# A transformer block on one core: the third mixer's centring, gates and norm logarithms written another way

## The chip, the core and the metric

The kernel runs on one core of a Trainium2 chip (trn2). The metric is the device time of one launch in microseconds, the median of several runs. A profile comes from one further execution of its own.

## The reference

One layer of a hybrid block on 256 tokens of width 2048, in float32. Cut to what matters here:

```
u = rms_norm(x) ; proj = u @ w_in              # q,k,v of two attentions, r,k,v and low ranks of the third mixer, 3 gates
y_a = stick_breaking_attention(...) ; y_b = forgetting_attention(...)
# third mixer: 16 heads of 64, per head and token a 64 x 64 state
kk    = k*k_k / max(sqrt(sum((k*k_k)**2)), 1e-12)          # norm over a head's 64 features
decay = exp(-exp(w_log)) ; a = sigmoid(a0 + ad @ a_up)
state = state*decay - (state @ kk)*(kk*a) + v*k            # token after token
y     = state @ r
y     = (y - mean(y)) * rsqrt(var(y) + eps) * ln_w + ln_b + bonus*v     # mean and var over the 64 features
m = g_a*(y_a @ P_a) + g_b*(y_b @ P_b) + g_c*(y_c @ P_c) ; x = x + rms_norm(m @ w_out)
x = x + rms_norm(relu(rms_norm(x) @ w_up)**2 @ w_down)
```

The subtraction of the mean over a head's features is linear, so the kernel applies it to v before the recurrence: a product of v with `cen`, the 128 x 128 matrix I - 1/64 inside each head's block.

## The kernel before

**Weights.** All weight matrices stream through SBUF as tiles of 128 x 1024 (`wraw`, L160; three buffers `raw`). Each tile is cut into a rounded high half `whi`, written by ScalarE (L173), and a low half `wlo`, the difference, written by VectorE (L175); three buffers each. TensorE multiplies both halves (`gemm`, L187, with lines L191, L195, L197; `tok`, L208, with lines L235 and L220), so every weight tile needs one step on each of the two vector engines before TensorE can read it. A rounded operand has the type fp32r ("hl", "whi", "cr" in the rows), an unrounded one f32; a product of unrounded operands stands in the trace as two passes of the same line, one of rounded operands as one. Activations are cut the same way by `split` (L253; ScalarE L256, VectorE L257). After a projection ScalarE moves half of a sum out of PSUM (L697) and VectorE adds the other half (L698).

**The mixer runs between the weight products.** The three mixers are one generator. Each `yield` gives a cost in vector time. `tick` (L137) is called once or twice in each weight tile, adds SHARE times its argument to a credit, and `step` (L116) runs pieces of the generator while the credit is positive. A plain number or ("go", cost) lets the next piece follow at once if credit is left. ("stage", cost, hold) ends the tick and lets nothing follow for `hold` ticks: it stands where TensorE's next products need what the vector engines have just been given. TensorE's order is the order in which this code calls it. The order of ScalarE, VectorE and GpSimd is made by the tile scheduler.

**The third mixer** (`rwkv_half`, L725) runs twice, for four pairs of heads each. In its order:

- sums of squares of k for the norm, two groups of two pairs (L745, L746, product `heads` in L100 and L101); of each group VectorE takes the maximum (L760), ScalarE the logarithm (L761) and the exponential (L762), each with a table load ahead of it; then five VectorE steps of a Newton correction (L764 to L769);
- `gates` (L776) for each pair: low-rank products (L783), three ScalarE steps (L791 to L793), VectorE's scan over the tokens of a chunk into `cs` (L794), two exponentials of it (L797 `ep`, L798 `em`), and operands for the recurrence on VectorE and GpSimd (L802 to L822);
- products per pair (L836, L840) and their masks (L845);
- centring of v (L857): per pair four products of 64 x 128 with unrounded v as the stationary and `cen` as the moving operand, 64 columns wide, in two column halves of the array;
- a triangular inverse on VectorE, 31 short pairs of steps between transposes (L876 to L893);
- the recurrence over four chunks (L928 to L964) and the head norm.

The constants lie in three tiles: `ident`; `cr`, which ScalarE writes rounded from `ones` (L447); and `con`, unrounded. `cen` lay in `con`.

Of the kernel before, what the change touches and what calls it, by code (L numbers as in the profile page):

```python
# [21 lines left out]
AHEAD = 1  # L22
SHARE = 0.88
HALF = 1024
# [18 lines left out]
_c = 0  # L43
for _n, _w in (("ident", 128), ("ones", 128), ("bones", 128), ("trig", 128), ("mst", 128),
               ("madd", 128), ("cen", 128), ("scm", 128), ("scan", 256)):
    CC[_n] = (_c, _w)
    _c += _w
NCON = _c
NR = 384


@with_exitstack
def hybrid_block(ctx, tc, xt, x, gains, params, consts, lora, gup, wst, out):
# [41 lines left out]
    def CR(name):  # L95
        c0 = CC[name][0] - 128
        return cr[:, c0:c0 + 128]
# [624 lines left out]
    def heads(ps, hi, lo):  # L722
        twice(ps, CR("bones"), *(t.rearrange("p a b -> p (a b)") for t in (hi, lo)))

    def rwkv_half(hf):  # L725
# [27 lines left out]
        for hi, lo in hls:  # L753
            pss.append(mps())
            heads(pss[-1], hi, lo)
        for i2, ps in enumerate(pss):
            ri = B6[:, 2 * i2:2 * i2 + 2, :]
            sc = B6[:, 4:6, :]
            sq = rp.tile([128, 2, T], F32, tag="AX", name=nm("sq"), bufs=5)
            V.tensor_scalar(sq, ps.rearrange("p (a b) -> p a b", a=2), 1e-24, None, ALU.max)  # L760
            A.activation(sc, sq, AF.Ln, scale=float(2.0 ** 20))  # L761
            A.activation(ri, sc, AF.Exp, scale=-0.5)  # L762
            yield 0.6
            V.tensor_scalar(ri, ri, 1024.0, None, ALU.mult)  # L764
# [11 lines left out]
        def gates(i, p):  # L776
# [16 lines left out]
            A.activation(lw, lw, AF.Identity, scale=CE, bias=cst[:, 0:1])  # L793
            V.tensor_tensor_scan(c, C("scan"), lw, 0.0, ALU.mult, ALU.add)  # L794
            c4 = c.rearrange("p (c t) -> p c t", c=4)
            G.memset(ep[:, :, 0:1], 1.0)
            A.activation(ep[:, :, 1:65], c4, AF.Exp)  # L797
            A.activation(em, c, AF.Exp, scale=-1.0)  # L798
            G.tensor_copy(ecol[:, i, :], ep[:, :, 64])
            yield 0.8  # L800
            kp = g1()
# [23 lines left out]
        for i, p in enumerate(PR):  # L825
# [25 lines left out]
            yield ("stage", 1.9, 3.5 if i == 0 else 2.0)  # L851

        pss = [mps(), mps()]
        for i, p in enumerate(PR):
            for cc in range(4):
                o = 256 * (i % 2) + 128 * (cc // 2)
                PE.matmul(pss[i // 2][64 * (cc % 2):64 * (cc % 2) + 64, o:o + 128], done[f"v{p}"][:, cc * 64:cc * 64 + 64],  # L857
                          C("cen"), start=True, stop=True)
        for i, p in enumerate(PR):
# [852 lines left out]
```

## Time and profile before

| | us |
|---|---|
| median of 3 runs (lowest to highest) | 1504.24 (1503.12 to 1506.56) |
| the profiled execution's own time | 1505.64 |
| its span, first to last instruction | 1503.8 |
| TensorE busy | 1489.7 |
| VectorE busy | 1206.8 |
| ScalarE busy | 938.4 |
| GpSimd busy | 91.1 |
| granted TensorE clock, mean of the span | 0.998 |

The third mixer's first half lies between about 200 and 410 us of the span, its second between about 427 and 660 us. In a timeline row the columns are start, length, engine, line, operation, operands, shape, count, and in brackets idle time just before and what ended it. A group's row ends in total busy time, mean ns of one, and idle time before. PE is TensorE, PEld its weight loads, DVE VectorE, ACT ScalarE, POOL GpSimd.

### The profile page before, as it was taken

The numbers are of one execution on the slowest core, as the hardware profiler recorded it, in microseconds if no ns is written. First come the engines' busy times: TensorE is split into PE (matmuls) and PEld (weight loads), VectorE is DVE, ScalarE is ACT, GpSimd is POOL, SyncE is SP. The second block draws the span as 40 slices with busy tenths as digits, with TensorE's granted clock in tenths as the row PEclk, the third lists the DMA queues.
The fourth block names the chain that finished last, engine by engine and source line by source line (L and its number), as shares of the span: only waits on it lengthen the run. The fifth ranks groups of instructions, "written<-read, shape, count | busy, mean of one in ns | idle before, by whom it ended". The sixth has DMA issues, their size and how long they took to land.

```text
span 1503.8 us, 22719 instructions
## 1 busy us (share of the span) xinstructions
PE 1489.7 (99%) x8384; PEld 1250.7 (83%) x8384; DVE 1206.8 (80%) x1677; ACT 938.4 (62%) x1435; POOL 91.1 (6%) x151
## 2 busy tenths in 40 slices
PE   9999999999999999999999999999999999999997
PEld 7888888887788887788888888888888888888886
DVE  7965679895688796476657788999899989999996
ACT  7665677545776445564445776776767666767663
POOL 0011003000001000000000000000000000000000
PEclk9999999999999999999999999999999999999999
DMA  8545445454445455345674768879888888889874
GB/s 284 202 150 178 151 158 169 155 182 162 157 167 173 150 192 189 135 165 195 226 243 161 261 179 256 252 223 286 243 269 239 225 279 258 249 259 261 256 216 149
DMA packets 107055, 312.19 MB, mean 208 GB/s; under 512 B 12352, under 2 KB 14400, under 8 KB 106944
## 3 DMA queue, kind: packets, MB, share of 16 engines
q1 hardware_dynamic: 96336, 279.35, 54.8%
q0 software_dynamic: 8064, 29.36, 10.5%
q10 hardware_dynamic: 2544, 2.03, 0.5%
q8 instruction: 66, 1.08, 0.3%
q14 instruction: 45, 0.37, 0.1%
HBM read 279.24 MB, written 2.10 MB: 187 GB/s over the span
## 4 chain that ended last, share of the span: by engine, by line
PE 94%; DVE 2%; ACT 1%; issue 1%; DMA 0%; SPq 0%; POOLq 0%; DVEq 0%; POOL 0%; ACTq 0%
PE gps L235 27%; PE gps L191 22%; PE gps L195 12%; PE gps L220 7%; PE mps L1430 3%; PE mps L1432 3%; PE mps L1431 3%; PE gps L1432 2%; PE gps L1430 2%; PE gps L1431 2%; PE gps L197 2%; DVE wlo L175 1%; PE mps L836 1%; PE gps L359 1%; PE gps L1219 1%
## 5 line engine op out<-in xcount | busy, mean ns | idle before, releaser
L175 DVE TENSOR_TENSOR wlo<-raw,whi 128x1024 fp32r<-128x1024 f32 x570 | 691.3, 1223 | 151.5 <-ACT whi L173 141.8
L173 ACT ACTIVATE whi<-raw 128x1024 fp32r<-128x1024 f32 x570 | 597.9, 1057 | 246.5 <-PE gps L235 71.7
L191 PE MATMUL gps<-pk,whi 128*128 128x512 f32 x1460 | 370.7, 392 | 1.0 <-ACT whi L173 0.8
L191 PEld LDWEIGHTS gps<-pk,whi 128*128 128x128 f32 x1460 | 270.6, 188 | 56.4 <-ACT whi L173 1.7
L235 PE MATMUL gps<-whi,pk 128*128 128x512 f32 x1004 | 253.5, 392 | 0.0
L195 PEld LDWEIGHTS gps<-pk,wlo 128*128 128x128 f32 x1561 | 212.8, 190 | 15.4 <-DVE wlo L175 0.5
L235 PEld LDWEIGHTS gps<-whi,pk 128*128 128x128 f32 x1004 | 186.4, 188 | 40.0 <-issue 1.0
L195 PE MATMUL gps<-pk,wlo 128*128 128x256 f32 x1561 | 218.0, 282 | 0.1
L235 PE MATMUL gps<-wlo,pk 128*128 128x512 f32 x502 | 138.1, 393 | 0.1
L235 PEld LDWEIGHTS gps<-wlo,pk 128*128 128x128 f32 x502 | 93.1, 188 | 20.0 <-DVE wlo L175 0.5
L1347 ACT ACTIVATE tmp<-gps 128x256 f32<-128x256 f32 x64 | 24.6, 385 | 105.2 <-PE gps L197 103.3
L1430 PE MATMUL mps<-whi,fm 128*128 128x512 f32 x224 | 88.6, 396 | 1.4 <-ACT whi L173 1.3
L1431 PE MATMUL mps<-whi,fm 128*128 128x512 f32 x224 | 87.7, 392 | 0.0
L1432 PE MATMUL mps<-wlo,fm 128*128 128x512 f32 x224 | 87.4, 390 | 0.0
L1410 POOL DMA_DIRECT2D raw<-raw x56 | 48.8, 872 | 571.9 <-DVE raw L1407 279.8
L1407 DVE TENSOR_TENSOR raw<-raw,raw 128x1024 f32<-128x1024 f32 x56 | 68.4, 1222 | 0.8
L1430 PE MATMUL gps<-whi,fm 128*128 128x512 f32 x168 | 65.8, 392 | 0.0
L1432 PE MATMUL gps<-wlo,fm 128*128 128x512 f32 x168 | 65.7, 391 | 0.0
L1431 PE MATMUL gps<-whi,fm 128*128 128x512 f32 x168 | 65.5, 390 | 0.0
L220 PE MATMUL gps<-whi,pk 128*128 128x512 f32 x224 | 60.8, 393 | 0.0
L1430 PEld LDWEIGHTS mps<-whi,fm 128*128 128x128 f32 x224 | 42.3, 189 | 9.7 <-ACT whi L173 3.5
L1432 PEld LDWEIGHTS mps<-wlo,fm 128*128 128x128 f32 x224 | 42.1, 188 | 9.4
(358 smaller groups left out, 1743.0 us busy)
## 6 DMA issues: line engine op xcount, KB each, us to landing
raw<-in_wst_dram SPq DMA_DIRECT2D x510, 512.0 KB, 4.3
raw<-raw POOLq DMA_DIRECT2D x56, 512.0 KB, 7.2
x<-in_xt_dram SPq DMA_DIRECT2D x8, 256.0 KB, 5.6
x<-in_x_dram SPq DMA_DIRECT2D x8, 256.0 KB, 5.5
raw<-in_wst_dram SPq DMA_DIRECT2D x6, 256.0 KB, 4.9
pk<-in_wst_dram SPq DMA_DIRECT2D x6, 256.0 KB, 5.1
g<-in_gains_dram SPq DMA_DIRECT2D x4, 256.0 KB, 5.0
pk<-in_gains_dram SPq DMA_DIRECT2D x4, 256.0 KB, 6.8
```

What stands on the lines that cost most here:

```text
L173: A.activation(hi, raw, AF.Copy)
L175: low = lambda: V.tensor_tensor(lo, raw, hi.bitcast(F32), ALU.subtract)
L191: PE.matmul(ps, hi[:, i * 128:i * 128 + 128], pks[i], start=first and i == 0, stop=False)
L195: PE.matmul(ps[:, 0:T], lo[:, i * 128:i * 128 + 128], pks[i][:, 0:T], start=False, stop=False)
L197: PE.matmul(ps, hi[:, (n - 1) * 128:n * 128], pks[n - 1], start=False, stop=True)
L220: PE.matmul(ps[tt], pks[k][:, c:c + 128], w[:, (k - k0) * 512:(k - k0) * 512 + 512], start=k == 0 and part == 0 and w is hl[0], stop=w is ...
L235: PE.matmul(ps[tt], pks[k][:, c:c + 128], w[:, (k - k0) * 512:(k - k0) * 512 + 512], start=k == 0 and part == 0 and w is hl[0], stop=False)
L1407: V.tensor_tensor(R[d, a], R[d, a], R[d, b], ALU.add)
L1410: G.dma_start(out=R[d, a], in_=R[d, b], accum_op=ALU.add)
L1430: PE.matmul(Q[f], a, w, start=d == d0 and i == 0, stop=False)
L1431: PE.matmul(Q[f], b, w, start=False, stop=False)
L1432: PE.matmul(Q[f], a, wl, start=False, stop=d == dn and i == 1)
```

## The change

Five edits in one:

1. SHARE goes from 0.88 to 0.93.
2. `cen` moves from the unrounded constants into the rounded tile, which grows from 384 to 512 columns.
3. Centring splits v of the four pairs into rounded high and low parts (L256, L257; one "go" or "stage" each), and multiplies both by the rounded `cen`: per pair four products of 128 x 128 over the array's full width, instead of four unrounded ones of 64 columns' width.
4. The norm takes the logarithms of both groups in one piece, the exponentials in the next, with a "stage" behind each, then both corrections.
5. In `gates` a "stage" of 0.7 stands between the scan and the exponentials; the 0.8 behind the exponentials is gone.

```diff
-SHARE = 0.88
+SHARE = 0.93
...
-NR = 384
+NR = 512
...
+        sc, sqs = B6[:, 4:6, :], []
         for i2, ps in enumerate(pss):
-            ri = B6[:, 2 * i2:2 * i2 + 2, :]
-            sc = B6[:, 4:6, :]
             sq = rp.tile([128, 2, T], F32, tag="AX", name=nm("sq"), bufs=5)
             V.tensor_scalar(sq, ps.rearrange("p (a b) -> p a b", a=2), 1e-24, None, ALU.max)
-            A.activation(sc, sq, AF.Ln, scale=float(2.0 ** 20))
-            A.activation(ri, sc, AF.Exp, scale=-0.5)
-            yield 0.6
+            A.activation(B6[:, 2 * i2:2 * i2 + 2, :], sq, AF.Ln, scale=float(2.0 ** 20))
+            sqs.append(sq)
+        yield ("stage", 1.0, 1)
+        A.activation(B6[:, 0:2, :], B6[:, 0:2, :], AF.Exp, scale=-0.5)
+        A.activation(B6[:, 2:4, :], B6[:, 2:4, :], AF.Exp, scale=-0.5)
+        yield ("stage", 0.1, 1)
+        for i2, sq in enumerate(sqs):
+            ri = B6[:, 2 * i2:2 * i2 + 2, :]
...
             V.tensor_tensor_scan(c, C("scan"), lw, 0.0, ALU.mult, ALU.add)
+            yield ("stage", 0.7, 0.7)
...
             G.tensor_copy(ecol[:, i, :], ep[:, :, 64])
-            yield 0.8
...
+        vs = []
+        for p in PR:
+            t = pair()
+            split(done[f"v{p}"], t.rearrange("p a b -> p (a b)"))
+            vs.append(t)
+            yield ("stage" if p == PR[3] else "go", 0.4, 2)
         pss = [mps(), mps()]
-        for i, p in enumerate(PR):
-            for cc in range(4):
-                o = 256 * (i % 2) + 128 * (cc // 2)
-                PE.matmul(pss[i // 2][64 * (cc % 2):64 * (cc % 2) + 64, o:o + 128], done[f"v{p}"][:, cc * 64:cc * 64 + 64],
-                          C("cen"), start=True, stop=True)
+        for i, t in enumerate(vs):
+            for b in range(2):
+                o = 256 * (i % 2) + 128 * b
+                for a in range(2):
+                    PE.matmul(pss[i // 2][:, o:o + 128], t[:, a, 128 * b:128 * b + 128], CR("cen"), start=a == 0,
+                              stop=a == 1)
```

The edits move the lines behind them: L761 and L762 of before are L760 and L763/L764 now, L797 is L802, L802 is L806, L857 is L868, L888 is L899, L893 is L904.

**Where ScalarE stands with the logarithms of the first half.** Before, the first group's (`sq_399`), around the high half `whi_418`; the second group's follow two high halves later:

```order
L173 ACTIVATE whi_409_2167<-raw_408_2165 128x1024
L699 ACTIVATE zp_403_2133<-tmp_402_2132,par_74 128x256
L761 ACT_TABLE_LOAD
L761 ACTIVATE b6_374_2037<-sq_399_2124 128x512
L173 ACTIVATE whi_418_2205<-raw_417_2203 128x1024
L762 ACT_TABLE_LOAD
L762 ACTIVATE b6_374_2037<-b6_374_2037 128x512
L697 ACTIVATE tmp_413_2194<-gps_404_2139 128x256
L173 ACTIVATE whi_421_2230<-raw_420_2228 128x1024
```

Now, both groups' between two high halves:

```order
L173 ACTIVATE whi_407_2144<-raw_406_2142 128x1024
L760 ACT_TABLE_LOAD
L760 ACTIVATE b6_374_2027<-sq_399_2114 128x512
L760 ACTIVATE b6_374_2027<-sq_400_2117 128x512
L763 ACT_TABLE_LOAD
L763 ACTIVATE b6_374_2027<-b6_374_2027 128x512
L764 ACTIVATE b6_374_2027<-b6_374_2027 128x512
L697 ACTIVATE tmp_402_2133<-gps_390_2073 128x256
L173 ACTIVATE whi_410_2171<-raw_409_2169 128x1024
```

The two groups' loads and steps were two pieces with high halves between and behind them; they are one piece now.

**ScalarE at the first pair's gates**, from the second group's logarithm or from the high half that takes its place. Before:

```order
L761 ACT_TABLE_LOAD
L761 ACTIVATE b6_374_2037<-sq_411_2177 128x512
L762 ACT_TABLE_LOAD
L762 ACTIVATE b6_374_2037<-b6_374_2037 128x512
L791 ACTIVATE lw_427_2256<-mps_425_2242,wah_123 128x256
L792 ACTIVATE tha_429_2258<-mps_426_2243,wah_123 128x256
L793 ACTIVATE lw_427_2256<-lw_427_2256,cst_116 128x256
L802 ACTIVATE g1_432_2279<-tha_429_2258,oka_124,wah_123 128x256
L697 ACTIVATE tmp_437_2291<-gps_416_2202 128x256
L797 ACTIVATE ep_431_2260<-cs_428_2257 128x4x64
L798 ACTIVATE em_430_2259<-cs_428_2257 128x256
L173 ACTIVATE whi_445_2324<-raw_444_2322 128x1024
```

Now:

```order
L173 ACTIVATE whi_442_2302<-raw_441_2300 128x1024
L795 ACTIVATE lw_427_2256<-mps_425_2242,wah_123 128x256
L796 ACTIVATE tha_429_2258<-mps_426_2243,wah_123 128x256
L797 ACTIVATE lw_427_2256<-lw_427_2256,cst_116 128x256
L806 ACTIVATE g1_432_2279<-tha_429_2258,oka_124,wah_123 128x256
L697 ACTIVATE tmp_437_2291<-gps_416_2202 128x256
L802 ACTIVATE ep_431_2260<-cs_428_2257 128x4x64
L803 ACTIVATE em_430_2259<-cs_428_2257 128x256
L173 ACTIVATE whi_446_2329<-raw_445_2327 128x1024
```

The second group's logarithm and exponential have left the piece; the exponentials of the scan (`cs`) stand behind the same step, L697, as before.

**VectorE at the end of the first triangular inverse**, up to the same weight tile (its low half is `wlo_691` before and `wlo_695` now; `Ti` and `tp` are the inverse's). Before:

```order
L175 TENSOR_TENSOR wlo_688_3475<-raw_686_3472,whi_687_3474 128x1024
L881 TENSOR_TENSOR tp_608_3042<-U_606_3040,Ti_607_3041 64x175
L883 TENSOR_TENSOR Ti_607_3041<-Ti_607_3041,tp_608_3042 64x7x25
L881 TENSOR_TENSOR tp_608_3042<-U_606_3040,Ti_607_3041 64x156
L883 TENSOR_TENSOR Ti_607_3041<-Ti_607_3041,tp_608_3042 64x6x26
L698 TENSOR_TENSOR tmp_681_3462<-gps_671_3402,tmp_680_3461 128x256
L881 TENSOR_TENSOR tp_608_3042<-U_606_3040,Ti_607_3041 64x135
L883 TENSOR_TENSOR Ti_607_3041<-Ti_607_3041,tp_608_3042 64x5x27
L175 TENSOR_TENSOR wlo_691_3494<-raw_689_3491,whi_690_3493 128x1024
```

Now:

```order
L175 TENSOR_TENSOR wlo_692_3488<-raw_690_3485,whi_691_3487 128x1024
L894 TENSOR_TENSOR Ti_611_3053<-Ti_611_3053,tp_612_3054 64x3x29
L892 TENSOR_TENSOR tp_612_3054<-U_610_3052,Ti_611_3053 64x60
L894 TENSOR_TENSOR Ti_611_3053<-Ti_611_3053,tp_612_3054 64x2x30
L892 TENSOR_TENSOR tp_612_3054<-U_610_3052,Ti_611_3053 64x31
L894 TENSOR_TENSOR Ti_611_3053<-Ti_611_3053,tp_612_3054 64x31
L899 STREAM_TRANSPOSE TW_679_3447<-Ti_611_3053 32x16x32 x2
L698 TENSOR_TENSOR tmp_685_3475<-gps_675_3418,tmp_684_3474 128x256
L904 STREAM_TRANSPOSE SC_423_2240<-Ti_611_3053 32x16x32
L175 TENSOR_TENSOR wlo_695_3508<-raw_693_3505,whi_694_3507 128x1024
```

The inverse is further on by four of its pairs of steps at this tile, and three of the four transposes behind it stand ahead of the low half.

4 lines of the change are left out of this document (2 added, 2 removed).

## The prediction

> **What bounds the kernel now.** I read the page's busy line first, then the chain that ended last, then TensorE's timeline for places where it stands still.
>
> ```profile
> PE 1489.7 (99%) x8384; PEld 1250.7 (83%) x8384; DVE 1206.8 (80%) x1677; ACT 938.4 (62%) x1435; POOL 91.1 (6%) x151
> PE 94%; DVE 2%; ACT 1%; issue 1%; DMA 0%; SPq 0%; POOLq 0%; DVEq 0%; POOL 0%; ACTq 0%
> ```
>
> TensorE is busy for 99% of the span and carries 94% of the chain. A change in the mixer can therefore act in three ways only: through the time its own products take on TensorE, through the few places where TensorE waits for a weight half, or by creating new ones. The profiled execution took 1505.64 us (span 1503.8 and 1.84 around it), 1.40 above the 1504.24 median of three runs. I work out differences and put them on the median. A measurement of this kernel tells about 0.2%, 3.0 us, from no change.
>
> The timeline of TensorE around 226 us shows the one clear wait inside the mixer's time. Columns are start, length, engine, line, operation.
>
> ```profile
> 200.69 0.40 PE L197 MATMUL gps<-pk,whi 128*128 128x512 f32 x1
> 200.93 1.32 PE L191 MATMUL gps<-pk,whi 128*128 128x512 f32 x5
> ...
> 219.71 2.00 PE L191 MATMUL gps<-pk,whi 128*128 128x512 f32 x8
> 221.55 1.12 PE L195 MATMUL gps<-pk,wlo 128*128 128x256 f32 x8
> ...
> 225.07 0.39 PE L197 MATMUL gps<-pk,whi 128*128 128x512 f32 x1
> 226.00 2.11 PE L191 MATMUL gps<-pk,whi 128*128 128x512 f32 x8 [0.54 <-ACT whi L173]
> 228.22 1.21 PE L195 MATMUL gps<-pk,wlo 128*128 128x256 f32 x8
> ```
>
> Undisturbed, L197 is followed by L191 after 0.24 us and eight L191 take 1.84. Here they take 0.93 and 2.22: TensorE loses 0.69 + 0.38 = 1.07 us. ScalarE before it:
>
> ```profile
> 216.44 1.28 ACT L761 ACT_TABLE_LOAD   x1
> 218.61 1.28 ACT L762 ACT_TABLE_LOAD   x1
> 219.91 0.63 ACT L762 ACTIVATE b<-b 128x512 f32<-128x512 f32 x1
> 224.27 0.42 ACT L797 ACTIVATE ep<-cs 128x256 f32<-128x256 f32 x1 [1.85 <-DVE cs L794]
> 224.91 1.04 ACT L173 ACTIVATE whi<-raw 128x1024 fp32r<-128x1024 f32 x1
> ```
>
> From 216.44 to 224.91 ScalarE makes no high half: two table loads, log and exponential of the second pair group, three tanh steps, and 1.85 us of standing still at L797 for VectorE's scan. Three buffers of whi do not cover 8.5 us. In the second half the same place costs less:
>
> ```profile
> 453.48 1.98 PE L235 MATMUL gps<-whi,pk 128*128 128x512 f32 x8
> 455.30 1.07 PE L235 MATMUL gps<-wlo,pk 128*128 128x512 f32 x4
> 456.20 1.98 PE L235 MATMUL gps<-whi,pk 128*128 128x512 f32 x8
> 458.25 1.21 PE L235 MATMUL gps<-wlo,pk 128*128 128x512 f32 x4
> ```
>
> Eight high products take 1.82, and 2.05 the second time; the four low ones also run 0.14 longer: 0.37 us, with VectorE late.
>
> **The change part by part.**
>
> *Logs in one step, gates in two.* The table loads and the wide steps are counted by these groups:
>
> ```profile
> L761 ACT ACT_TABLE_LOAD x4 | 5.1, 1283 | 0.1
> L762 ACT ACT_TABLE_LOAD x4 | 5.1, 1283 | 0.1
> ```
>
> Each half loses one load at L761 and one at L762, 4 x 1.283 = 5.1 us of ScalarE in all. In the new order both logs and both exponentials stand three high halves earlier as one block: 2 x 1.28 + 4 x 0.55 (the 0.63 at 219.91 less the overlap with the next) = 4.8 us without a high half, then L697. The block of 8.5 us falls to the three tanh steps, L806, L697, a wait for the scan and two exponentials, about 4 us. TensorE takes 2.72 us a tile (453.48 to 456.20 in the rows above), and beside the tile in use two more fit the three buffers, 5.4 us: both blocks fit into that, so the 1.07 us should go. If ScalarE enters the first block less than 4.8 us ahead, that block shows instead. The step between scan and exponential does not do what its name says at the first gate: in the order nothing but L697 stands between, so L802 can still wait for the scan, with one high half queued behind it. It has less ahead of it. In the second half, VectorE no longer waits for an exponential at the first operation of the second group, so I count the 0.37 as gone too. Term: **-1.4**, bounds 0 and -1.5; a loss is left out, since the same steps run with fewer loads.
>
> The Trainium skill, page "ScalarE: Activation LUTs", section "Table sets: the hidden batching unit", speaks against this part: one set holds log and exponential, so a log followed by an exponential needs one load. By it the grouping would remove no load, the block would stay, and the sum would be 1.4 us higher. The rows decide: every log and every exponential here has its own load of 1283 ns.
>
> *Centring.* The row of the old products, with their neighbours, and two neighbours of the new ones:
>
> ```profile
> 280.19 1.30 PE L191 MATMUL gps<-pk,whi 128*128 128x512 f32 x5
> 281.43 1.97 PE L857 MATMUL mps<-con,g 128*64 128x128 f32 x32
> 283.32 0.73 PE L191 MATMUL gps<-pk,whi 128*128 128x512 f32 x2
> 283.90 1.10 PE L195 MATMUL gps<-pk,wlo 128*128 128x256 f32 x8
> 284.83 0.40 PE L191 MATMUL gps<-pk,whi 128*128 128x512 f32 x1
> ...
> 241.62 0.66 PE L840 MATMUL mps<-ident,At 128*128 128x128 f32 x4
> 242.03 0.36 PE L100 MATMUL mps<-hl,cr 128*128 128x256 f32 x1
> ```
>
> Old, per half: 16 products of full precision in 32 passes, 281.43 to 283.32, 1.89 us. Entering and leaving the 64-wide form costs 0.10 (five L191 in 1.24 against 5 x 0.227, 1.82 / 8 above) and 0.13 (two in 0.58 against 0.45): 2.12. New: 16 rounded products, 128 wide, 128 columns, nothing to enter. No row shows that form. Below stands half of L195, which has the same weights and 256 columns: 0.93 / 8 = 0.116, halved 0.058, 0.93 us in all. Above stands the old price of a full-width product, two 64-wide ones of two passes: 1.89 / 8 = 0.236, 3.78 us. Nearest are L195 itself and the one-pass 128-column L840, 0.41 / 4 = 0.103; both load 128 columns of weights each time. I take 0.11: 1.76 us, a gain of 0.36 per half. Term: **-0.7**, bounds -2.4 and +3.3.
>
> *Work added for it.* Four copies and four differences per half:
>
> ```profile
> L256 ACT ACTIVATE pk<-g 128x256 fp32r<-128x256 f32 x8 | 3.0, 404 | 0.9 <-DVE g L1005 0.9
> L257 DVE TENSOR_TENSOR pk<-g,pk 128x256 fp32r<-128x256 f32 x8 | 3.3, 418 | 0.5 <-ACT pk L256 0.5
> ```
>
> ScalarE gets 8 x 0.404 = 3.2 us, less than the loads it loses. VectorE gets 4 x 0.418 = 1.7 us per half, just ahead of the triangular inverse, where it has no room. TensorE's centring group stands behind the last difference, which the order puts ahead of the low half of the tile where TensorE meets the group; a tile's 2.72 us covers it, and without that cover the next weight tile would wait behind the group. How full VectorE is:
>
> ```profile
> 278.00:336.00 58.00, 58.00 (x398) 50.03 (x397) 56.56 (x109) 29.76 (x47) 0.59 (x6) 1.00 0.48 163
> 511.00:571.80 60.80, 60.80 (x295) 50.05 (x294) 58.54 (x105) 27.77 (x38) 0.00 (x0) 1.00 0.48 161
> ```
>
> The columns after the length are TensorE, weight load, VectorE, ScalarE: VectorE is busy for 97% and 96% of the two inverses.
>
> *The larger share.* At 0.93 the mixer's steps come 5.7% sooner, counted in weight tiles, and TensorE's mixer groups move by at most two tiles. The total of mixer work is the same, so nothing is gained at the end, where TensorE has gate products to do anyway. But inside an inverse more VectorE work falls between two low halves. I added the rows of VectorE's order between low halves, at the durations of their lines in the trace: up to the tile whose low half is wlo_691 before and wlo_695 now, VectorE has been given 6.6 us more since the gates, as three transposes now stand ahead of it. Three tiles later all but 1.3 of it is given back.
>
> ```profile
> L888 DVE STREAM_TRANSPOSE TW<-Ti 32x512 f32<-32x512 f32 x4 | 4.6, 1188 | 0.0
> L893 DVE STREAM_TRANSPOSE SC<-Ti 32x512 f32<-32x512 f32 x8 | 8.7, 1083 | 0.1
> ...
> 277.89 1.29 DVE L845 TENSOR_TENSOR SC<-mps,con 128x512 f32<-128x512 f32 x2 [1.05 <-PE mps L836]
> ...
> 325.36 1.21 DVE L175 TENSOR_TENSOR wlo<-raw,whi 128x1024 fp32r<-128x1024 f32 x1
> ...
> 328.43 1.07 PE L235 MATMUL gps<-wlo,pk 128*128 128x512 f32 x4
> ```
>
> Three transposes are 3.4 us of the 6.6. Against it stand the idle time of 1.05 us ahead of the inverse, which can be filled, and TensorE's group of L836, which lies one tile earlier, so that VectorE begins the inverse 2.7 us sooner: 2.85 us are left. Today that low half (325.36) is done at 326.57 and first read at 328.43, 1.86 us ahead. So TensorE waits 2.85 - 1.86 = 1.0 us: **+1.0**, bounds 0 (a step that ScalarE or a buffer held up anyway) and 6.6 - 1.86 = 4.7 (nothing of the idle time can be used). The second inverse has more idle time ahead of it, from 475 to 510 us:
>
> ```profile
> DVE wlo L175 <- ACT whi L173: 7.7, 5, 1.9
> ```
>
> Five gaps of 7.7 us in all can take the extra, and I count nothing there. Vector steps outside the inverses, the 64 KB more of rounded constants and GpSimd, at 6%, cost nothing: idle time of those engines covers them.
>
> Sum: 1505.64 - 1.4 - 0.7 + 1.0 = 1504.5 for such an execution; on the median 1504.24 - 1.1 = **1503.1**.
>
> **The rivals.** *VectorE becomes the bound in both inverses* (slower). For it: 97% busy, and a low half only 1.86 us ahead. Against it: the extra is transient. It decides where the idle time and the earlier start can't be used: then the first inverse costs 4.7 by itself, 1504.24 - 1.4 - 0.7 + 4.7 = 1506.8, and 1511.5 if the second costs as much again.
> *Small rounded products cost two passes.* For it: every unrounded product here does. Against: L195 and L840. 1504.24 - 1.4 + 3.3 + 1.0 = 1507.1.
> *They cost what their columns cost*, 0.058 to 0.08. For it: L195 costs half of L191 (0.116 against 0.227), so columns set the price there. Against: L840. With 0.07: 2 x (2.12 - 1.12) = 2.0, and no wait in the inverse: 1504.24 - 1.4 - 2.0 = 1500.8. The Trainium skill, page "TensorE: Matmul & The Clock Gate", section "Back-to-back issue gap", gives about 81 ns for 128 columns in a stream of loads and products; by it the gain of this term would be 2 x (2.12 - 1.30) = 1.6 us, an estimate. No run here shows that form.
> *The step does not part scan and exponential*, and the 1.07 us wait stays, at this tile or another, so that only the 0.37 goes. For it: the order, where L802 still follows L697. Against: the block ahead of it is gone. 1504.24 - 0.4 - 0.7 + 1.0 = 1504.1.
>
> **How the numbers follow.** Forecast (1501.6 to 1504.6) 0.42; VectorE bound 0.17, two passes 0.12, cost by columns 0.13, no parting 0.16. The range leaves out the outer part of the VectorE rival and a little at each end of the others: 1500.4 to 1507.2. Faster by over 0.2% (below 1501.2): most of the column rival and a tail of the forecast, 0.17. Slower (above 1507.2): half of the VectorE rival and of the two-pass one, and a little for a wait that I did not see, 0.17. The rest, 0.66, lies within.
>
> **What would show it.** L191 after L197 near 226 us at 0.24 and no `<-ACT whi` there; four table loads fewer, two each at the new lines; the centring group at 1.7 to 1.8 us for 16 records, 0.9 or 3.8 for the rivals; low halves in the first inverse read within 1 us of their end, with TensorE idle `<-DVE wlo L175` near 325 to 335. Wrong would be TensorE waits of over 1 us anywhere between 280 and 570, or a mixer group that waits for its operands.

## The result and the profile after

The changed kernel takes 1507.64 us (median of 12 runs, 1506.05 to 1512.30), the kernel before 1504.57 beside it (12 runs, 1503.12 to 1507.51). The ratio is **1.0021**, 95% interval 1.0011 to 1.0031: 3.1 us slower, where 1.1 us faster was forecast, and 0.4 us above the range. The profiled execution took 1508.15 us with a span of 1506.4, against 1505.64 and 1503.8 before.

The busy line of the page hardly moves. TensorE's waits do: a list of them, with the microseconds in all, the number and the longest.

```profile
PE 1489.8 (99%) x8352; PEld 1250.0 (83%) x8352; DVE 1209.1 (80%) x1685; ACT 934.7 (62%) x1439; POOL 88.0 (6%) x151
...
PE gps L235 <- DVE wlo L175: 2.0, 2, 1.7
PE mps L467 <- DVE a L462: 1.2, 1, 1.2
```

The kernel before has neither of the two waits. I price each wait by starts: the time from one product's start to the next, less what the same pair takes undisturbed. TensorE at the start, near 226 us and near 458 us:

```profile
35.12 0.39 PE L197 MATMUL gps<-pk,whi 128*128 128x512 f32 x1
36.75 0.70 PE L467 MATMUL mps<-a,cr 128*128 128x256 f32 x2 [1.24 <-DVE a L462]
...
225.68 0.40 PE L197 MATMUL gps<-pk,whi 128*128 128x512 f32 x1
225.91 2.00 PE L191 MATMUL gps<-pk,whi 128*128 128x512 f32 x8
227.75 0.52 PE L195 MATMUL gps<-pk,wlo 128*128 128x256 f32 x3
...
457.57 1.07 PE L235 MATMUL gps<-wlo,pk 128*128 128x512 f32 x4
458.48 1.98 PE L235 MATMUL gps<-whi,pk 128*128 128x512 f32 x8
460.30 1.07 PE L235 MATMUL gps<-wlo,pk 128*128 128x512 f32 x4
```

L191 follows L197 after 0.23 us near 226, and the eight take 1.84: the 1.07 us are gone. At 458 the eight high products take 1.82 and the four low ones 0.91: the 0.37 us are gone too. ScalarE ahead of the first of these places:

```profile
216.90 1.06 ACT L173 ACTIVATE whi<-raw 128x1024 fp32r<-128x1024 f32 x1 [0.77 <-DMA raw<-in_wst_dram]
222.49 0.42 ACT L802 ACTIVATE ep<-cs 128x256 f32<-128x256 f32 x1 [1.58 <-DVE cs L798]
223.12 1.05 ACT L173 ACTIVATE whi<-raw 128x1024 fp32r<-128x1024 f32 x1
```

It still stands still for 1.58 us at L802 for the scan, where it was 1.85: the new step hardly parts scan and exponential at the first gate. But the stretch without a high half is 5.2 us long (217.96 to 223.12) instead of 8.5, as the second group's logarithm and exponential have left it. At the start L467 begins 1.63 us after L197, where it took 0.24 before (35.95 to 36.19): 1.39 us new. VectorE there, after and then before; L462 adds up the squares that L467 reads:

```profile
33.64 0.69 DVE L462 TENSOR_TENSOR a<-a 128x512 f32<-128x512 f32 x1
34.86 1.23 DVE L175 TENSOR_TENSOR wlo<-raw,whi 128x1024 fp32r<-128x1024 f32 x1 [0.54 <-ACT whi L173]
36.01 0.69 DVE L462 TENSOR_TENSOR a<-a 128x512 f32<-128x512 f32 x1
```

```profile
34.12 1.48 DVE L462 TENSOR_TENSOR a<-a 128x512 f32<-128x512 f32 x2
35.52 1.22 DVE L175 TENSOR_TENSOR wlo<-raw,whi 128x1024 fp32r<-128x1024 f32 x1
```

The last addition now stands behind one more low half, which itself waits for its high half. The centring, the first inverse, the second group of logarithms and the second inverse on TensorE:

```profile
279.41 1.54 PE L191 MATMUL gps<-pk,whi 128*128 128x512 f32 x6
280.79 1.90 PE L868 MATMUL mps<-cr,hl 128*128 128x128 f32 x16
282.52 0.69 PE L191 MATMUL gps<-pk,whi 128*128 128x512 f32 x2
283.05 1.11 PE L195 MATMUL gps<-pk,wlo 128*128 128x256 f32 x8
...
326.57 1.98 PE L235 MATMUL gps<-whi,pk 128*128 128x512 f32 x8
330.24 1.19 PE L235 MATMUL gps<-wlo,pk 128*128 128x512 f32 x4 [1.69 <-DVE wlo L175]
...
436.76 1.07 PE L235 MATMUL gps<-wlo,pk 128*128 128x512 f32 x4
438.17 2.11 PE L235 MATMUL gps<-whi,pk 128*128 128x512 f32 x8 [0.34 <-ACT whi L173]
...
539.98 1.07 PE L220 MATMUL gps<-whi,pk 128*128 128x512 f32 x4
541.23 0.73 PE L220 MATMUL gps<-wlo,pk 128*128 128x512 f32 x2 [0.19 <-DVE wlo L175]
...
565.74 1.54 PE L235 MATMUL gps<-whi,pk 128*128 128x512 f32 x6
567.64 1.20 PE L235 MATMUL gps<-wlo,pk 128*128 128x512 f32 x4 [0.35 <-DVE wlo L175]
```

The sixteen rounded products take 1.73 us from 280.79 to 282.52. The six before them take 1.38 instead of 1.36, the two behind 0.53 instead of 0.45: 1.83 in all, against 2.12. The eight products at 326.57 last 3.67 us until the next start instead of 1.81: 1.86 lost, and 0.37 is lost at another low half of this inverse, near 305: 2.23 in all. Near 437 it is 1.41 instead of 0.91, in the second inverse 1.25 instead of 0.91 and 1.90 instead of 1.36.

The sum: 1.39 + 2.23 + 0.50 + 0.88 new, 1.07 + 0.37 removed, 2 x 0.29 for the centring, **+2.98 us**. The spans differ by 2.6 and the medians by 3.07. That the three agree so closely is partly luck. From the products just ahead of L467 to the end of the mixer the changed trace loses 3.8 us, 0.8 more than this list holds; and the two traces also differ by 0.8 us in the first 35 us (less now), by 1.1 near 1200 us (less now) and by 0.8 between 1310 and 1360 us (more now), which I can't put down to any edit. The list tells where most of the time in the mixer went, not yet which part of the change sent it there.

### The profile page after: what moved, and what is told of

Read it like the earlier page. It is cut to its first block, busy times and chain, and to the rows that moved or that the text cites. A ratio compares the mean times of both kernels' runs of the same rounds, so it can differ in the third digit from the quotient of the medians.

```text
span 1506.4 us, 22659 instructions
## 1 busy us (share of the span) xinstructions
PE 1489.8 (99%) x8352; PEld 1250.0 (83%) x8352; DVE 1209.1 (80%) x1685; ACT 934.7 (62%) x1439; POOL 88.0 (6%) x151
## 4 chain that ended last, share of the span: by engine, by line
PE 88%; DVE 6%; issue 2%; ACT 2%; DMA 1%; ACTq 0%; SPq 0%; DVEq 0%; POOLq 0%; POOL 0%
PE gps L235 23%; PE gps L191 21%; PE gps L195 12%; PE gps L220 6%; PE mps L1441 3%; PE mps L1442 3%; PE mps L1443 3%; DVE wlo L175 3%; PE gps L1443 2%; PE gps L1441 2%; PE gps L1442 2%; PE gps L197 1%; DVE tp L892 1%; DMA raw<-in_wst_dram 1%; DVE Ti L894 1%
## 5 line engine op out<-in xcount | busy, mean ns | idle before, releaser
L191 PE MATMUL gps<-pk,whi 128*128 128x512 f32 x1460 | 370.1, 392 | 0.2 <-ACT whi L173 0.2
L191 PEld LDWEIGHTS gps<-pk,whi 128*128 128x128 f32 x1460 | 270.5, 188 | 55.3 <-ACT whi L173 0.9
L195 PEld LDWEIGHTS gps<-pk,wlo 128*128 128x128 f32 x1561 | 212.6, 190 | 16.1 <-DVE wlo L175 1.3
L195 PE MATMUL gps<-pk,wlo 128*128 128x256 f32 x1561 | 218.2, 282 | 0.2 <-DVE wlo L175 0.2
```

Source lines behind the costliest of these rows:

```text
L191: PE.matmul(ps, hi[:, i * 128:i * 128 + 128], pks[i], start=first and i == 0, stop=False)
L195: PE.matmul(ps[:, 0:T], lo[:, i * 128:i * 128 + 128], pks[i][:, 0:T], start=False, stop=False)
```

## The experiments

My theory had three parts: the start's wait comes from the place of the centring matrix among the constants, the waits in the inverses from the larger share, and the edits on logarithms and gates are a gain. The rival put the waits in the inverses down to the work that the centring adds to VectorE. Neither held fully. Each run has its own runs of the kernel before on the same chip; medians in us:

| run | this | before | ratio, 95% interval |
|---|---|---|---|
| b_const | 1505.50 | 1503.67 | 1.0013 (1.0004 to 1.0022) |
| b_share93 | 1509.22 | 1503.67 | 1.0037 (1.0025 to 1.0050) |
| b_cen | 1516.82 | 1503.67 | 1.0087 (1.0073 to 1.0101) |
| share88 | 1514.85 | 1503.67 | 1.0075 (1.0063 to 1.0088) |
| b_lg | 1502.01 | 1504.37 | 0.9982 (0.9973 to 0.9991) |
| a_sep | 1507.09 | 1504.37 | 1.0020 (1.0011 to 1.0029) |
| free88 | 1506.89 | 1504.37 | 1.0020 (1.0012 to 1.0029) |
| a_sep_pool | 1506.60 | 1504.37 | 1.0017 (1.0008 to 1.0025) |
| b_lg93 | 1510.04 | 1504.41 | 1.0038 (1.0025 to 1.0051) |
| a_sep_free88 | 1506.01 | 1504.41 | 1.0012 (1.0004 to 1.0021) |
| a_sep_pool_free88 | 1506.19 | 1504.41 | 1.0013 (1.0004 to 1.0022) |
| a_sep_pool90 | 1506.85 | 1504.41 | 1.0019 (1.0010 to 1.0027) |
| b_lg_splits | 1501.78 | 1504.20 | 0.9989 (0.9979 to 0.9998) |
| t_noyield88 | 1506.30 | 1504.20 | 1.0019 (1.0010 to 1.0028) |
| t_blg_h1 | 1503.67 | 1504.20 | 0.9996 (0.9987 to 1.0004) |
| b_lg_full | 1501.87 | 1504.20 | 0.9986 (0.9977 to 0.9995) |

### The four parts one by one

**b_const**, the constants alone:

```diff
-NR = 384
+NR = 512      # and "cen" listed behind "trig", as in the change
```

> The kernel before with one edit: the centring matrix stands among the rounded constants (512 columns rounded instead of 384), SHARE, centring products and logs as before. Theory (the start's wait comes from this move alone): in the first 40 us VectorE's last square-sum addition stands behind one more low half, TensorE waits about 1.2 us for it near 36 us and the first L467 starts about 1.6 us after the last L197; everything else as before, so span and time +1.2 to +1.5 us against the kernel before. Rival (the wait came from a late transfer or from another edit): no wait there, time within 0.3 us of before.

TensorE waits 1.3 us for L462, near 36 us, and the time rises by 1.8. The place of the matrix makes the start's wait by itself.

**b_share93**, the share alone:

```diff
-SHARE = 0.88
+SHARE = 0.93
```

> The kernel before with SHARE 0.93 and nothing else. Theory (the larger share alone crowds VectorE in the inverses): TensorE waits in the first inverse for low halves, 1.5 to 3 us in all, in the second one 0.3 to 1; the waits near 226 and 458 us stay in some form, 1 to 1.4; no wait at the start; in all +1.5 to +3 us. Rival (the waits come from the vector work of the new centring, the four differences a half): waits in the inverses under 0.5 us in all, time within 0.5 us of before.

TensorE in the first inverse, and a row of the table of windows there; its last columns are the granted clock, the DMA share and GB/s:

```profile
326.21 1.98 PE L235 MATMUL gps<-whi,pk 128*128 128x512 f32 x8
331.08 1.76 PE L235 MATMUL gps<-wlo,pk 128*128 128x512 f32 x4 [2.89 <-DVE wlo L175]
332.77 1.08 PE L898 MATMUL mps<-TW,SC 32*32 32x32 f32 x64
333.78 3.78 PE L235 MATMUL gps<-whi,pk 128*128 128x512 f32 x8
337.36 1.52 PE L235 MATMUL gps<-wlo,pk 128*128 128x512 f32 x4
338.73 1.98 PE L235 MATMUL gps<-whi,pk 128*128 128x512 f32 x8
```

```profile
332.00:338.00 6.00, 6.00 (x76) 4.42 (x76) 2.52 (x3) 2.96 (x6) 0.00 (x0) 0.50 0.86 268
```

The wait is 3.06 us by starts (4.87 instead of 1.81). After it the granted clock is 0.50: eight high products take 3.58 us (333.78 to 337.36) instead of 1.81, the four low ones 1.37 instead of 0.91. No wait is left in the second inverse, and there is none near 305. Near 226 us TensorE still loses 1.03, now at L195, which waits for a low half. So the share crowds the first inverse, and the time rises by 5.5, more than expected because of the clock.

**b_cen**, rounded constants and the whole centring edit at the old share:

> The kernel before with the rounded constants and the centring as rounded products of split values, at SHARE 0.88, logs and gates as before. Theory: start's wait +1.4, centring -0.8, the first inverse waits up to 1 us, the wait near 226 us stays; since the added steps put the end of the mixer about 7 us of TensorE's work later, a wait of 0 to 2 us may show up at its end; in all +0.5 to +3 us. Rival (the four differences crowd the inverses, not the share): waits of 2 to 3 us in the first inverse and 0.5 or more in the second, in all +3 to +4 us.

**share88**, the changed kernel with `SHARE = 0.88`:

> The changed kernel with SHARE back at 0.88. Theory: start's wait stays (+1.4), waits near 226 and 458 us stay away (-1.4), centring -0.8, half a microsecond behind the second half's block of logs, under 0.7 us of waits in the two inverses together, and 0 to 2 us at the mixer's end: -0.5 to +2 us against the kernel before, 1 to 3 us below the changed kernel if the end doesn't wait. Rival (differences, not share): the first inverse still waits 2 us or more and the time is that of the changed kernel within 0.5 us.

Both are far slower than either theory said, most of all at the end of the mixer. TensorE in share88, where the last group of the mixer waits for ScalarE and the branch's products for the mixer's result:

```profile
659.28 0.61 PE L220 MATMUL gps<-wlo,pk 128*128 128x512 f32 x2
661.88 0.49 PE L100 MATMUL mps<-hl,cr 128*128 128x512 f32 x1 [1.99 <-ACT hl L994]
...
676.70 0.49 PE L220 MATMUL gps<-whi,pk 128*128 128x512 f32 x1 [0.55 <-ACT pk L256]
```

The four new steps charge the planner 0.4 each and hold it for two tiles, and in TensorE's order the mixer's last group moves from 556 us of weight products to 564. There the waits and the lower clock behind them come to 5.8 us in share88 (from 659.28 to 670.43), and the two waits for the branch near 677 us cost 1.8 more; in b_cen one wait there is 3.9. The inverses wait too, at the old share: 0.48 and 0.71 in the first of share88, 0.81 and 1.30 in the second, and 0.49, 0.75, 0.85 and 1.72 in b_cen. The 3.3 us of share88 are far above the 0.7 that my theory gave it. The larger share of the change is what hides this end: it brings the last group to 552.

### Logarithms and gates alone, and the start

**b_lg**, the kernel before with the two hunks on logarithms and gates:

> The kernel before with the two edits on logarithms and gates alone, SHARE 0.88 and the old centring. Theory: TensorE's waits near 226 and 458 us go (1.07 and 0.37), half a microsecond comes behind the second half's block of logarithms near 437 us, the start, the inverses and the end stay as before: 0.8 to 1.4 us below the kernel before. Rival (the gates' parting did nothing, the waits went with the larger share): the wait near 226 us stays at about 1, time within 0.3 us of before or above it.

2.4 us faster (1.4 to 4.1 by the interval; the waits removed are 1.44, and what else is gained isn't shown). The waits near 226 and 458 us are gone. The two hunks were not run apart. Near 437 there is no wait, against what I expected. The two longest of TensorE's waits that are left, 1.1 and 0.5 us, lie outside the mixer.

**a_sep**, the changed kernel with a rounded copy of the matrix in a tile of its own:

```diff
-NR = 512      # "cen" back behind "madd"
+NR = 384
+    crc = rp.tile([128, 128], F32R, name="crc")
+        A.activation(crc, C("cen"), AF.Copy)        # when the third mixer begins
```

> The changed kernel with the centring matrix back among the unrounded constants (384 columns rounded at the start, as before) and a rounded copy of its own, made by one ScalarE step of 128 columns when the third mixer begins. Theory (the move of the matrix reorders the start): the wait of about 1.2 us at L467 near 36 us goes, the rest stays: 1.2 to 1.8 us below the changed kernel, so 1.2 to 2 above before. Rival (something else delays the start, a transfer for instance): the wait stays and the time is that of the changed kernel within 0.4 us.

The wait at L467 is gone from the trace, and the profiled execution took 1505.48 instead of 1508.15. On the medians it shows as 0.55, less than expected and within the scatter.

### Is it the added work?

**free88** is share88 with uncharged steps:

```diff
-            yield ("stage" if p == PR[3] else "go", 0.4, 2)
+            yield ("stage" if p == PR[3] else "go", 0.0, 1)
```

> The changed kernel at SHARE 0.88, and the four new steps of the centring charge the planner nothing (cost 0 in place of 0.4 each, a hold of one tile in place of two): the same instructions, given out earlier, so that the mixer's last group stands at TensorE's 556 us of matrix work as before, and not at 564. Theory (the charges, not the work, put the mixer's end too late): the 5.6 us of waits between 655 and 680 us go, the waits of the second inverse stay or shrink (1 to 2), start +1.4, logs +0.5, centring -0.8, waits near 226 and 458 us gone: 0.5 to 2.5 us above before, 8 or more below the changed kernel at SHARE 0.88. Rival (the added copies and differences themselves delay the end): 4 us or more of waits there, 8 or more above before.

The mixer's end no longer waits, and 8.7 us against share88 are back: the charges and the longer hold made that wait. In the inverses 1.15 us are left in the first (0.51 + 0.64) and 1.56 in the second (0.39 + 0.74 + 0.43).

**a_sep_pool** is a_sep with the differences on GpSimd:

```diff
-            split(done[f"v{p}"], t.rearrange("p a b -> p (a b)"))
+            A.activation(t[:, 0, :], done[f"v{p}"], AF.Copy)
+            G.tensor_tensor(t[:, 1, :], done[f"v{p}"], t[:, 0, :].bitcast(F32), ALU.subtract)
```

> The changed kernel with the rounded centring matrix as a copy of its own (no wait at the start) and the four differences a half of the split values made by GpSimd instead of VectorE: 1.7 us less VectorE work ahead of each inverse, SHARE 0.93 as changed. Theory (share and differences both fill VectorE there): the waits in the first inverse fall from 2.2 us to 0.3 to 1, in the second from 0.9 to under 0.3; GpSimd's 0.8 to 0.9 us a difference does not delay the centring group by more than 1 us: 1 to 2 us below the same kernel with VectorE's differences, about the time of before. Rival (the share alone fills it, what stands ahead of the inverse does not matter): the first inverse waits 2 us or more as it did.

Nothing moves: 0.37 and 1.81 in the first inverse, as 0.39 and 1.80 in a_sep; 0.85 in the second, as 0.88. My theory that the differences count is wrong here.

**b_lg93**, b_lg with `SHARE = 0.93`:

> The kernel before with the edits on logarithms and gates and SHARE 0.93, old centring, old constants. Theory (the share by itself crowds VectorE in the first inverse, whatever stands ahead of it): waits of 3 to 3.5 us for low halves near 328 us, under 0.4 in the second inverse, 0.3 to 0.6 near 436 us behind the block of logarithms; 3.5 to 4.5 us above the same kernel at 0.88, 1 to 2.5 above before. Rival (with the logarithms moved VectorE is ahead by then, and the waits of 2 us in the changed kernel come from its centring): under 1.5 us of waits in the first inverse, at most the time of before.

3.05 in the first inverse, none in the second: the theory's side, with no centring edit in it. Near 437 us there is no wait here either; that one stands only in the three traces that have both the share of 0.93 and the new centring (changed kernel, a_sep, a_sep_pool). The time is 8.0 above b_lg, of which this wait explains 3.05 and the lower clock behind it 1.8. The profiled execution loses 3.5 more at four places between 1030 and 1210 us, where no edit acts; the cause of that stays open.

**a_sep_free88** (all edits at 0.88, matrix apart, uncharged), **a_sep_pool_free88** (the differences on GpSimd as well) and **a_sep_pool90** (charged as in the change, share 0.90):

> All edits at SHARE 0.88, the rounded centring matrix as a copy of its own (no reordering at the start), the centring's steps uncharged. Theory: no wait at 36 us; waits of 1.1 us in the first inverse and 1.5 in the second as with the matrix among the constants; none at the mixer's end; between 0.5 below and 1 above before, and 2 to 3 above the kernel with logarithms and gates alone. Rival (the waits in the inverses follow from the late start, since everything after it is shifted): inverses at under 0.5 us in all, 1.5 to 3 below before.

> The same with the four differences a half on GpSimd. Theory (at 0.88 the differences on VectorE are what makes the inverse start late): waits under 0.5 us in the first inverse and under 0.6 in the second, 1.5 to 3 below before and 0.3 to 0.9 below the kernel with logarithms and gates alone, the gain of the centring itself. Rival (as at 0.93 they don't matter, and the later place of the centring among the weight tiles does): waits of 1.1 and 1.5 us stay, time within 0.4 us of the same kernel with VectorE's differences.

> The matrix as a copy of its own, differences on GpSimd, the steps charged as in the change, SHARE 0.90: the mixer's last group stands at 556 us of TensorE's matrix work as before, the first inverse lies over 50.6 us of it (51.1 before, 48.4 changed). Theory (what an inverse waits is set by the room between its low halves): 0.3 to 1.5 us in the first inverse, under 1 in the second, none at the end: 1.5 below to 0.5 above before. Rival (any share above 0.88 brings the wait near 328 us in full): 2 us or more there, 0.5 to 2 above before.

Waits in the first and second inverse: 1.15 and 1.52 (a_sep_free88), 1.10 and 1.58 (a_sep_pool_free88), 1.13 and 1.67 (a_sep_pool90). GpSimd changes nothing at 0.88 either; moving the share to 0.90 shifts the waits, with nearly the same sum. None comes down to the kernel before: they are 1.6 to 2.4 us above it. The waits of the first are those of its theory and those of the second those of its rival, but the times of the first and the third lie above what either side forecast. With VectorE's differences ruled out twice, the question was what else of the centring acts.

### Work, place or order

**b_lg_splits** does the copies and differences and reads none of them, with the old products:

```diff
+        for p in PR:
+            t = pair()
+            split(done[f"v{p}"], t.rearrange("p a b -> p (a b)"))
         pss = [mps(), mps()]
```

> The kernel with logarithms and gates alone (SHARE 0.88, no waits in the inverses), and the four copies and four differences a half of v made ahead of the centring, uncharged; the old products stay, the split halves are not read. Theory (the order of VectorE's inverse steps makes the waits, not the added work): VectorE's order in the inverses is that of the kernel without the splits, waits under 0.4 us in each inverse, time within 0.5 us of it. Rival (the work of the copies and differences makes them): 1 us or more in the first inverse and 1.5 in the second, 2 to 3 us above it.

No wait in either inverse, 1501.78 us: the work of the splits costs nothing.

**t_noyield88**, the reverse: splits and rounded products at the old place, without steps of their own (a_sep at 0.88 with the `yield` taken out).

> All edits at SHARE 0.88, the rounded matrix as a copy of its own, the splits and the rounded products at the old place of the centring, without steps of their own. TensorE's groups stand where they stood before. VectorE's order has six pairs of inverse steps and a transpose ahead of a low half in the first inverse where the kernel with the old products has four. Theory (rounded products make the tile scheduler pack the inverse's steps ahead of low halves): waits of 0.7 to 2.5 us in the two inverses together, 0 to 2 us above the kernel with logarithms and gates alone. Rival (the later place of the centring made them): no waits, 0.3 to 0.9 below it.

The waits are back: 0.30 and 1.65 in the first inverse, 0.20 and 1.42 in the second, and the time is 4.5 above b_lg_splits. (Another 1.1 us of the difference between the two traces lies near 1200 us, where no edit acts.) In the code the two runs differ by the products, which now read the rounded halves, and by the copy of the matrix. The copy is not it: free88 without it and a_sep_free88 with it wait alike, 1.15 each in the first inverse and 1.56 and 1.52 in the second. TensorE's groups stand where they stand in b_lg_splits. What differs is VectorE. Its rows near the end of the first inverse, each with TensorE's beside them, in t_noyield88 and then in b_lg:

```profile
327.55 1.21 DVE L175 TENSOR_TENSOR wlo<-raw,whi 128x1024 fp32r<-128x1024 f32 x1
328.68 2.28 DVE L900 STREAM_TRANSPOSE TW<-Ti 32x512 f32<-32x512 f32 x2
330.87 2.12 DVE L905 STREAM_TRANSPOSE SC<-Ti 32x512 f32<-32x512 f32 x2
333.02 1.23 DVE L175 TENSOR_TENSOR wlo<-raw,whi 128x1024 fp32r<-128x1024 f32 x1
...
330.84 1.98 PE L235 MATMUL gps<-whi,pk 128*128 128x512 f32 x8
334.31 0.96 PE L235 MATMUL gps<-wlo,pk 128*128 128x512 f32 x3 [1.49 <-DVE wlo L175]
```

```profile
327.84 1.23 DVE L175 TENSOR_TENSOR wlo<-raw,whi 128x1024 fp32r<-128x1024 f32 x1
328.98 2.22 DVE L892 STREAM_TRANSPOSE TW<-Ti 32x512 f32<-32x512 f32 x2
331.11 2.12 DVE L897 STREAM_TRANSPOSE SC<-Ti 32x512 f32<-32x512 f32 x2
333.26 1.23 DVE L175 TENSOR_TENSOR wlo<-raw,whi 128x1024 fp32r<-128x1024 f32 x1
...
330.11 1.98 PE L235 MATMUL gps<-whi,pk 128*128 128x512 f32 x8
331.92 1.07 PE L235 MATMUL gps<-wlo,pk 128*128 128x512 f32 x4
```

In both, four transposes of 1.1 us stand between two low halves, and a low half ends 5.4 to 5.5 us after the one before it. Counted from the program's start in VectorE's order, 105 low halves stand ahead of the transposes in b_lg and 104 in t_noyield88. One more low half is in hand in b_lg when the block begins, and TensorE reads it at 331.92. In t_noyield88 the first low half behind the block is the one that TensorE needs.

The other traces say the same. I count the low halves that VectorE has made when the first of the four transposes begins, less the weight tiles that TensorE has begun (its high products, eight a tile), and compare this lead with that of b_lg:

| inverse | traces | lead against b_lg, tiles | waits in the inverse, us |
|---|---|---|---|
| first | before, b_const, b_lg, b_lg_splits, t_blg_h1, b_lg_full | 0 to 0.1 more | none |
| first | the seven with the new products at 0.88 or 0.90 | 0.4 to 0.6 less | 1.1 to 2.0 |
| first | the five at 0.93 | 1.0 less | 2.2 to 3.1 |
| second | the eight without the new products, two of them at 0.93 | 0 to 0.25 less | none over 0.15 |
| second | the ten with the new products | 0.5 to 0.9 less | 0.85 to 2.6 |

"New products" are those that read the rounded halves. So in the second inverse, and between 304 and 311 us too, a wait stands in the ten traces with these products and in no other, whatever the share; at the first inverse's transposes the larger share makes it as well. How long it is there also depends on how many of the four transposes stand ahead of the next low half: 0.6 to 0.75 us with three and 1.65 with four at 0.88 and 0.90, 1.8 to 1.9 with three and 3.05 with four at 0.93.

**t_blg_h1** adds `yield ("stage", 0.0, 1)` ahead of the old centring and nothing else:

> The kernel with logarithms and gates alone and one added line: the centring is held for one tile more, no other work. VectorE's order then has six and a half pairs of inverse steps and a transpose between two low halves. Theory (the order alone is enough): waits of 0.5 to 1.5 us in the first inverse, 0 to 1 in the second. Rival (it takes the centring's own work or its rounded products): under 0.3 us in all, time of the kernel without the line.

No wait. Many inverse steps between two low halves are not enough: 105 low halves stand ahead of the transposes here too. The median is 1.7 above b_lg, with runs from 1501.80 to 1506.58; the span of the profiled execution is 0.7 above. I leave that open.

**b_lg_full** uses full-width unrounded products:

```diff
-            for cc in range(4):
-                o = 256 * (i % 2) + 128 * (cc // 2)
-                PE.matmul(pss[i // 2][64 * (cc % 2):64 * (cc % 2) + 64, o:o + 128], done[f"v{p}"][:, cc * 64:cc * 64 + 64],
+            for b in range(2):
+                o = 256 * (i % 2) + 128 * b
+                PE.matmul(pss[i // 2][:, o:o + 128], done[f"v{p}"][:, 128 * b:128 * b + 128],
                           C("cen"), start=True, stop=True)
```

> The kernel with logarithms and gates alone, its centring as eight unrounded products of full width a half instead of sixteen of half width: 16 passes of 128 columns where there were 32, as many as the rounded products take, with no copy, no difference and no rounded matrix. Theory (a pass costs the 0.109 us that the rounded one does, its weights set the price, and VectorE's order stays near that of before): 1.7 to 1.9 us a half instead of 2.1, no new waits, 0.3 to 0.9 us below the kernel with the old products. Rival (a pass of full width costs twice that of half width): 3.8 us a half, 3 us above it.

TensorE in b_lg_full:

```profile
278.14 1.54 PE L191 MATMUL gps<-pk,whi 128*128 128x512 f32 x6
279.52 1.95 PE L861 MATMUL mps<-con,g 128*128 128x128 f32 x16
281.22 0.71 PE L191 MATMUL gps<-pk,whi 128*128 128x512 f32 x2
281.77 0.99 PE L195 MATMUL gps<-pk,wlo 128*128 128x256 f32 x7
```

1.70 + 0.02 + 0.10 = 1.82 us a half unrounded, where the rounded ones of the change take 1.83: the gain of the centring comes from the full width, and rounding adds nothing to it. There are no new waits, and 1501.87 us is below both the kernel before and the changed one. b_lg, b_lg_splits and b_lg_full can't be told apart by their intervals.

## Why the prediction was wrong

**Three steps failed: in "The larger share … +1.0" the 1.05 us of idle time that was taken off; the price of nothing for the second inverse, where the new products act; and "the 64 KB more of rounded constants … cost nothing".** Term by term, forecast and measured in the two profiled executions:

| term | forecast, us | measured, us |
|---|---|---|
| logarithms and gates | -1.4 | -1.44, and +0.50 near 437 us |
| centring's products | -0.7 | -0.58 |
| larger share, first inverse's transposes | +1.0 | +1.86 |
| near 305 us and second inverse | 0 | +0.37 and +0.88 |
| constants | 0 | +1.39 |
| sum | -1.1 | +2.98 |

- *Logs and gates, -1.4.* Right where it was placed: 1.07 and 0.37 are gone, and b_lg alone gains 2.4. The block that was to fall to about 4 us fell to 5.2, still within the 5.4 of two tiles. (Of its "three tanh steps" the third is a scaling; nothing hangs on it.) In the changed kernel 0.50 comes back near 437 us, where high halves queue behind two table loads, the logarithms and the exponentials. The condition was in the prediction ("enters the first block less than 4.8 us ahead, that block shows instead") but got no price. It takes the larger share and the new centring together; neither alone shows it (b_lg93, share88).
- *Centring, -0.7.* Right: 1.83 us a half instead of the forecast 1.76, -0.6 in all. Both rivals on its price fell. The text tied the gain to rounding; b_lg_full shows that width alone gives it.
- *The share, +1.0 in the first inverse.* The mechanism was right: a low half late, behind three transposes. The size was not. VectorE's rows of the changed kernel, the last masks ahead of the inverse and that low half:

```profile
275.06 1.28 DVE L849 TENSOR_TENSOR SC<-mps,con 128x512 f32<-128x512 f32 x2
...
328.99 1.19 DVE L175 TENSOR_TENSOR wlo<-raw,whi 128x1024 fp32r<-128x1024 f32 x1
```

From 275.06 to the end of the low half at 330.18 VectorE takes 55.12 us, where it took 48.68 (277.89 to 326.57): 6.44 more, near the 6.6 that was counted. It starts 2.83 us sooner, near the 2.7. But that is all: the prediction took off another 1.05 for the idle time ahead of the inverse, and the sooner start already uses that time: the row at 275.06 has no idle time before it any more. So the low half is 6.44 - 2.83 = 3.61 us late and not 2.85; less the slack of 1.86, which held, 1.75 is left, and 1.86 was measured. Alone the share costs 3.05 there (b_share93, b_lg93), with all four transposes ahead of the low half. In the changed kernel the new products act at this place too (0.6 to 0.75 at 0.88), so that the 1.86 isn't the share's alone.

- *The second inverse, "I count nothing there".* For the share this was right: alone it leaves no wait there. The 0.88, and the 0.37 near 305 us, come with the centring's new products. The prediction looked for a price of the centring in added work on VectorE and in a late group on TensorE. The added work does cost nothing (b_lg_splits). But with products that read the rounded halves the tile scheduler gives VectorE's inverse steps out about one low half earlier (t_noyield88). Why it does so was not tried.
- *Constants.* Counted as 64 KB and idle engines; they cost 1.39 us at the start, since the order of two steps of VectorE changed. I had looked only at the third mixer's part of the order.
- *"The total of mixer work is the same, so nothing is gained at the end."* Wrong, though no term of the sum hung on it: with the charges of the new steps and without the larger share the end of the mixer loses 7.6 us (share88). The change as it is charged needs its larger share, and pays for it in the first inverse.
- *Rivals.* VectorE as the bound came nearest, with 3.1 us in both inverses where its price was 4.7 to 9.4. "The step does not part" was right in its premise, since L802 still waits 1.58 us for the scan, and wrong in its price: the wait of 1.07 us went all the same, as the stretch without a high half had become shorter (5.2 us instead of 8.5).

## What to carry to other kernels

When a scheduler makes the order of an engine, an edit acts through that order as much as through its work: compare the whole order, from the first instruction, and look where a long block (here four transposes, 4.4 us) lies among the pieces that the busiest engine reads, and how many of these are in hand. When a sum takes off both idle time and an earlier start, ask whether the one is made of the other. Test the parts of a change alone; here one part was a gain of 2.4 us and the others lost it and more. Before splitting values to make products cheaper, try the full width of the array with the values as they are.

## What the runs showed of the hardware

A wait can cost twice. After the 2.89 us in b_share93 the granted clock fell to 0.50, and the next products lost 3.3 us more (0.78 on the four low products at 331.08, 0.32 on the 64 small ones, which take 0.69 in b_lg, and 1.77 and 0.46 on the eight and four that follow). In share88 a wait of 1.99 with another of 0.23 just behind it was enough:

```profile
664.00:670.00 6.00, 6.00 (x16) 4.30 (x16) 1.91 (x3) 4.72 (x5) 0.00 (x0) 0.50 0.26 87
```

The waits of 1.69 in the changed kernel and 1.49 in t_noyield88 left the clock at 1.00. Of the eighteen traces five have a stretch at half the clock in mid-span, and they are the five with a wait of TensorE of 1.99 us or more. The Trainium skill, page "TensorE: Matmul & The Clock Gate", in its part on the HAM clock gate, has the clock at half after an idle window of about 3.4 us. The half is what the trace shows; the gaps that brought it on were shorter here.
